# Weighted sum of two expert outputs: tiles of 12 tokens in four buffers in place of 8 in six

## The chip, the core and the metric

The kernel runs on one core of a Trainium2 chip. A core has engines that run beside each other, each with its own queue of instructions in a fixed order: TensorE (PE, not used here), VectorE (DVE), ScalarE (ACT), GpSimd (POOL) and SyncE (SP). Sixteen DMA engines move data between the HBM and the on-chip memory of 128 partitions. The transfers of this kernel are issued from SyncE's queue (q1 in the profile) and from ScalarE's queue (q10); both feed the same sixteen engines. The metric is the time of one execution in microseconds of device time.

## The reference

There are 16 x 1024 tokens; each has two expert outputs of 512 float32 numbers and two weights.

```python
batch, seq, hidden, n_experts, k = 16, 1024, 512, 8, 2
expert_outputs  # (batch, seq, k, hidden) float32, random
combine_weights # (batch, seq, k) float32, random

def reference(expert_outputs, combine_weights):
    weights = combine_weights[..., np.newaxis]
    return np.sum(expert_outputs * weights, axis=2).astype(np.float32)
```

So each output row is `w0 * x0 + w1 * x1`. 67.1 MB of expert outputs are read, 33.6 MB are written, and little is computed on each number.

## The kernel before

The 16384 tokens are spread over 128 partitions, 128 tokens each (`per`). A tile is J = 8 tokens of every partition, so there are 16 tiles, numbered by g. In the first 15 tiles a partition owns 120 consecutive tokens (`main`), whose inputs are 120 x 4 KB = 480 KB apart from those of the next partition; a tile takes 8 consecutive tokens of it, a row of 32 KB. The last tile is laid out by itself: 8 consecutive tokens of each partition, 32 KB apart. `rows` (lines 33 to 37) makes these two views, for inputs, weights and outputs.

The weights are loaded once at the start by two small transfers (lines 53 to 56), the 120 tokens' part from SyncE and the last tile's from ScalarE. One dummy activation on line 59 makes ScalarE load its function table early.

Then, for each tile:

- Line 65: SyncE loads the tile into a buffer `et` of 32 KB per partition. The pool has six such buffers, so the load of tile g+6 is held until the store of tile g has read the buffer.
- Line 70: VectorE multiplies all 16 rows of 512 (8 tokens, two experts) with their weights, in place, in one instruction of 8192 elements per partition.
- Line 71: VectorE adds the two halves of each token and writes the 4096 sums packed into the first half of the same buffer (`ot`).
- Line 72: ScalarE's queue issues the store, one row of 16 KB per partition.

The last tile (lines 75 to 88) is cut by token. ScalarE multiplies the token's first row with its weight (line 77), and VectorE multiplies the second row and adds (line 80). The store is issued from SyncE (line 88), behind all the loads.

The program is written with a tile framework that sets the semaphores and, from its own plan, the order of each engine's instructions. That order is mostly the order of the code, with one exception that matters at the end: on ScalarE two activations of the last tile stand ahead of the stores of tiles 13 and 14, and on VectorE the last multiplies and adds are grouped in pairs. Each queue is served in order: an instruction that waits holds back all behind it on its engine.

A load or a store of a tile is split over the sixteen DMA engines, eight partitions each. A partition's row is one packet. Where both queues have packets for an engine, it takes them in turn.

Of the kernel before, what the change touches and what calls it, by code (L numbers as in the profile page):

```python
# [1 line left out]

# [4 lines left out]


@with_exitstack
def kernel(  # L10
    ctx: ExitStack,
    tc: tile.TileContext,
    expert_outputs: bass.AP,
    combine_weights: bass.AP,
    out: bass.AP,
):

    nc = tc.nc  # L20
    b, s, k, h = expert_outputs.shape
    assert k == 2
    n = b * s
    P = nc.NUM_PARTITIONS
    per = n // P
    assert per * P == n
    J = 8
    main = per - J
    eo = expert_outputs.rearrange("b s k h -> (b s) (k h)")
    cw = combine_weights.rearrange("b s k -> (b s) k")  # L30
    o = out.rearrange("b s h -> (b s) h")

    def rows(x):

        a = x[0 : P * main, :].rearrange("(p t) f -> p t f", p=P)
        b = x[P * main : n, :].rearrange("(p t) f -> p t f", p=P)
        return lambda t, c: a[:, t : t + c, :] if t < main else b[:, t - main : t - main + c, :]

    eo, cw, o = rows(eo), rows(cw), rows(o)

    dt = mybir.dt.float32
    mult = mybir.AluOpType.mult
    add = mybir.AluOpType.add
    copy = mybir.ActivationFunctionType.Copy

    last = per // J - 1

    wpool = ctx.enter_context(tc.tile_pool(name="w", bufs=1))
    ipool = ctx.enter_context(tc.tile_pool(name="in", bufs=6))

    wt = wpool.tile([P, per * k], dt)

    for eng, t, c in ((nc.sync, 0, main), (nc.scalar, main, J)):
        eng.dma_start(  # L54
            out=wt[:, k * t : k * (t + c)].rearrange("p (t k) -> p t k", k=k), in_=cw(t, c)
        )

    warm = wpool.tile([P, 1], dt)
    nc.scalar.activation(out=warm, in_=nc.const_aps.tensor(1.0, (P, 1), dt), func=copy)  # L59

    for g in range(per // J):
        et = ipool.tile([P, J, k * h], dt)

        ot = et.rearrange("p j f -> p (j f)")[:, 0 : J * h].rearrange("p (j f) -> p j f", f=h)
        nc.sync.dma_start(out=et, in_=eo(g * J, J))  # L65
        if g < last:

            wb = wt[:, g * J * k : (g + 1) * J * k].unsqueeze(2).to_broadcast([P, J * k, h])
            ek = et.rearrange("p j (k h) -> p (j k) h", k=k)
            nc.vector.tensor_tensor(out=ek, in0=ek, in1=wb, op=mult)  # L70
            nc.vector.tensor_tensor(out=ot, in0=et[:, :, 0:h], in1=et[:, :, h : 2 * h], op=add)  # L71
            nc.scalar.dma_start(out=o(g * J, J), in_=ot)  # L72
            continue

        for i in range(J):
            t = g * J + i
            nc.scalar.activation(  # L77
                out=et[:, i, 0:h], in_=et[:, i, 0:h], func=copy, scale=wt[:, 2 * t : 2 * t + 1]
            )
            nc.vector.scalar_tensor_tensor(  # L80
                out=ot[:, i, :],
                in0=et[:, i, h : 2 * h],
                scalar=wt[:, 2 * t + 1 : 2 * t + 2],
                in1=et[:, i, 0:h],
                op0=mult,
                op1=add,
            )
        nc.sync.dma_start(out=o(g * J, J), in_=ot)


# [1 line left out]
_INS = ['expert_outputs', 'combine_weights']  # L92
_OUTS = [((16, 1024, 512), 'float32')]


# [23 lines left out]
```

## Time and profile before

| What | Value |
|---|---|
| Median of 3 runs | 240.47 us (240.06 to 240.93) |
| Profiled execution, its own time | 240.47 us |
| Profiled execution, span of the trace | 238.5 us |
| DMA engines, busy share by queue | 68.0% (q1) and 30.9% (q10) |
| VectorE busy | 201.3 us (84%) |
| ScalarE busy | 6.6 us (3%) |
| Transferred | 100.80 MB in 4896 packets, mean 423 GB/s |
| Load of a tile, median from issue to landing | 47.2 us |
| Store of a tile from ScalarE, median from issue to landing | 25.0 us |

The span is what the trace covers, from the first to the last instruction of the execution; the device time is about 2 us longer. A share of the span near 100% on the DMA engines means that they hardly rest. The time from issue to landing includes the time in the queue, so it is many times what the transfer itself takes.

### The profile page before, as it was taken

Reading aid. Unit: us, or ns where it says so; the run is one execution under the profiler, and the core shown is the slowest. Engines: PE = TensorE matmul, PEld = TensorE weight load, DVE = VectorE, ACT = ScalarE, POOL = GpSimd, SP = SyncE. Lnnn points to the kernel's source line nnn. Section 1 sums busy time; section 2 is a strip of 40 time slices with the busy share of each in tenths; the row PEclk is TensorE's granted clock in tenths of the full one; section 3 lists DMA queues with packets and bytes.
Section 4 is the critical chain, followed back from the end, with each engine's and each line's share of the span. In section 5 each row is a group of like instructions: output and inputs, shape, how many; then the busy total and the mean of one; then the engine's idle time right before and its main releaser. Section 6 shows DMA issues by size and latency. Waiting matters only on the chain.

```text
span 238.5 us, 170 instructions
## 1 busy us (share of the span) xinstructions
DVE 201.3 (84%) x38; ACT 6.6 (3%) x10; POOL 0.2 (0%) x4
## 2 busy tenths in 40 slices
DVE  0079999999999998989979799797927999899950
ACT  2000000000000000000000000000000000000530
POOL 0000000000000000000000000000000000000000
DMA  8999989999999999999999999999999999999997
GB/s 286 440 434 429 412 352 437 442 440 451 423 445 393 440 442 440 415 431 467 398 437 473 412 407 473 434 401 431 448 409 426 478 437 401 440 437 404 393 440 308
DMA packets 4896, 100.80 MB, mean 423 GB/s; under 512 B 672, under 2 KB 800, under 8 KB 800
## 3 DMA queue, kind: packets, MB, share of 16 engines
q1 hardware_dynamic: 2592, 69.33, 68.0%
q10 hardware_dynamic: 2304, 31.47, 30.9%
HBM read 67.24 MB, written 33.55 MB: 423 GB/s over the span
## 4 chain that ended last, share of the span: by engine, by line
DMA 65%; DVE 29%; ACT 1%; ACTq 0%; DVEq 0%; issue 0%; SPq 0%
DMA et<-in_expert_outputs_dram 44%; DMA out_dram<-et 21%; DVE et L70 18%; DVE et L71 10%; ACT et L77 1%; DVE et L80 1%; DVEq L114 0%; ACTq L114 0%; SPq L54 0%; ACTq L72 0%; SPq L65 0%; DVEq L80 0%; DVEq L70 0%
## 5 line engine op out<-in xcount | busy, mean ns | idle before, releaser
L70 DVE TENSOR_TENSOR et<-et,wt 128x8192 f32<-128x8192 f32 x15 | 130.4, 8690 | 28.1 <-DMA et<-in_expert_outputs_dram 28.1
L71 DVE TENSOR_TENSOR et<-et 128x4096 f32<-128x4096 f32 x15 | 66.2, 4423 | 0.4
L77 ACT ACTIVATE et<-et,wt 128x512 f32<-128x512 f32 x8 | 5.1, 710 | 220.7 <-DMA et<-in_expert_outputs_dram 218.8
L80 DVE SCALAR_TENSOR_TENSOR et<-et,wt 128x512 f32<-128x512 f32 x8 | 5.6, 748 | 0.2
L59 ACT ACT_TABLE_LOAD x1 | 1.3, 1283 | 1.2 <-PEq L103 1.2
L59 ACT ACTIVATE warm<-const-float32-1.0 128x1 f32<-128x1 f32 x1 | 0.2, 204 | 0.0
L103 POOL MEMSET const-bfloat16-1.0<- 128x1 bf16 x1 | 0.1, 102 | 0.0
L103 POOL MEMSET const-uint8-127<- 128x1 uint8 x1 | 0.1, 102 | 0.0
L103 POOL MEMSET const-float32-0.0<- 128x1 f32 x1 | 0.1, 99 | 0.2 <-issue 0.2
L103 POOL MEMSET const-float32-1.0<- 128x1 f32 x1 | 0.1, 99 | 0.0
## 6 DMA issues: line engine op xcount, KB each, us to landing
et<-in_expert_outputs_dram SPq DMA_DIRECT2D x16, 4096.0 KB, 47.2
out_dram<-et ACTq DMA_DIRECT2D x15, 2048.0 KB, 25.0
out_dram<-et SPq DMA_DIRECT2D x1, 2048.0 KB, 7.6
wt<-in_combine_weights_dram SPq DMA_DIRECT2D x1, 120.0 KB, 2.2
wt<-in_combine_weights_dram ACTq DMA_DIRECT2D x1, 8.0 KB, 2.3
```

The lines of the kernel that those rows point to most:

```text
L59: nc.scalar.activation(out=warm, in_=nc.const_aps.tensor(1.0, (P, 1), dt), func=copy)
L70: nc.vector.tensor_tensor(out=ek, in0=ek, in1=wb, op=mult)
L71: nc.vector.tensor_tensor(out=ot, in0=et[:, :, 0:h], in1=et[:, :, h : 2 * h], op=add)
L77: nc.scalar.activation(out=et[:, i, 0:h], in_=et[:, i, 0:h], func=copy, scale=wt[:, 2 * t : 2 * t + 1])
L80: nc.vector.scalar_tensor_tensor(out=ot[:, i, :], in0=et[:, i, h : 2 * h], scalar=wt[:, 2 * t + 1 : 2 * t + 2], in1=et[:, i, 0:h], op0=mul ...
L103: nc = _bacc.Bacc("TRN2", target_bir_lowering=False, num_devices=1)
```

## The change

Tiles have 12 tokens and there are ten of them; an eleventh, the last, has 8 and is laid out as before. `main` stays 120 and the input rows of neighbouring partitions stay 480 KB apart. A tile's load row becomes 48 KB and its store row 24 KB. The pool has four buffers of 48 KB in place of six of 32 KB, the same 192 KB in all.

The first nine tiles are computed as before, with instructions of 12288 and 6144 elements (lines 72 and 73 of the new file), and stored from ScalarE's queue (line 74). In tile 9 ScalarE multiplies the first rows of its 12 tokens one by one (line 80), VectorE multiplies the second rows in one instruction of 6144 elements (line 95) and adds in another (line 96), and the store is issued from SyncE (line 97). Tile 10 is computed like the old last tile, token by token (lines 80 and 84), and stored from SyncE (line 97).

In the built program, ScalarE's queue holds the stores of tiles 0 to 7, then eight of tile 9's activations, then the store of tile 8, then the other four and the eight of tile 10. SyncE's queue holds all eleven loads, then the stores of tiles 9 and 10. VectorE's order is that of the code, without the pairs.

```diff
-    J = 8
-    main = per - J
+    J, LAST = 12, 8
+    main = per - LAST
+    assert main % J == 0
...
-    last = per // J - 1
+    last = main // J
...
-    ipool = ctx.enter_context(tc.tile_pool(name="in", bufs=6))
+    ipool = ctx.enter_context(tc.tile_pool(name="in", bufs=4))
...
-    for eng, t, c in ((nc.sync, 0, main), (nc.scalar, main, J)):
+    for eng, t, c in ((nc.sync, 0, main), (nc.scalar, main, LAST)):
...
-    for g in range(per // J):
+    for g in range(last + 1):
         et = ipool.tile([P, J, k * h], dt)
...
-        nc.sync.dma_start(out=et, in_=eo(g * J, J))
-        if g < last:
+        t0, c = g * J, J if g < last else LAST
+        nc.sync.dma_start(out=et[:, 0:c], in_=eo(t0, c))
+        if g < last - 1:
...
-            nc.scalar.dma_start(out=o(g * J, J), in_=ot)
+            nc.scalar.dma_start(out=o(t0, c), in_=ot)
             continue
 
-        for i in range(J):
-            t = g * J + i
+
+        for i in range(c):
+            t = t0 + i
             nc.scalar.activation(
                 out=et[:, i, 0:h], in_=et[:, i, 0:h], func=copy, scale=wt[:, 2 * t : 2 * t + 1]
             )
-            nc.vector.scalar_tensor_tensor(
-                out=ot[:, i, :],
-                in0=et[:, i, h : 2 * h],
-                scalar=wt[:, 2 * t + 1 : 2 * t + 2],
-                in1=et[:, i, 0:h],
-                op0=mult,
-                op1=add,
-            )
-        nc.sync.dma_start(out=o(g * J, J), in_=ot)
+            if g == last:
+                nc.vector.scalar_tensor_tensor(
+                    out=ot[:, i, :],
+                    in0=et[:, i, h : 2 * h],
+                    scalar=wt[:, 2 * t + 1 : 2 * t + 2],
+                    in1=et[:, i, 0:h],
+                    op0=mult,
+                    op1=add,
+                )
+        if g < last:
+            w1 = wt.rearrange("p (t k) -> p t k", k=k)[:, t0 : t0 + c, 1:2]
+            x1 = et[:, :, h : 2 * h]
+            nc.vector.tensor_tensor(out=x1, in0=x1, in1=w1.to_broadcast([P, c, h]), op=mult)
+            nc.vector.tensor_tensor(out=ot, in0=et[:, :, 0:h], in1=x1, op=add)
+        nc.sync.dma_start(out=o(t0, c), in_=ot[:, 0:c])
```

## The prediction

> **What bounds the kernel now.** I read the DMA queues and the DMA share first, then the groups by line, then the waits of SyncE, then the end of the timeline. The DMA queues (queue, packets, MB, share of 16 engines' span):
>
> ```profile
> q1 hardware_dynamic: 2592, 69.33, 68.0%
> q10 hardware_dynamic: 2304, 31.47, 30.9%
> HBM read 67.24 MB, written 33.55 MB: 423 GB/s over the span
> ```
>
> The shares add to 98.9%: the 16 DMA engines are the bound. In four stretches (length, busy time of the engines, granted clock, DMA share, GB/s):
>
> ```profile
> 0.00:2.40 2.40, 0.00 (x0) 1.25 (x1) 0.20 (x4) 1.00 0.53 135
> 2.40:219.00 216.60, 190.56 (x29) 0.24 (x2) 0.00 (x0) 1.00 1.00 430
> 219.00:237.30 18.30, 10.79 (x10) 5.12 (x8) 0.00 (x0) 1.00 0.95 402
> 237.30:238.50 1.20, 0.00 (x0) 0.00 (x0) 0.00 (x0) 1.00 0.00 0
> ```
>
> From 2.4 to 219 us no engine rests. Only 2.4 us ahead, 1.2 us behind and 5% of the last 18.3 us (0.9 us) are not transfer. The groups by line (busy us, mean ns, idle before):
>
> ```profile
> L70 DVE TENSOR_TENSOR et<-et,wt 128x8192 f32<-128x8192 f32 x15 | 130.4, 8690 | 28.1 <-DMA et<-in_expert_outputs_dram 28.1
> L71 DVE TENSOR_TENSOR et<-et 128x4096 f32<-128x4096 f32 x15 | 66.2, 4423 | 0.4
> L77 ACT ACTIVATE et<-et,wt 128x512 f32<-128x512 f32 x8 | 5.1, 710 | 220.7 <-DMA et<-in_expert_outputs_dram 218.8
> L80 DVE SCALAR_TENSOR_TENSOR et<-et,wt 128x512 f32<-128x512 f32 x8 | 5.6, 748 | 0.2
> ```
>
> VectorE needs 8.69 + 4.42 = 13.1 us a tile and waits only for loads. The timeline shows the rate of the transfers, one tile in 14.54 us, and the end:
>
> ```profile
> 122.16 8.69 DVE L70 TENSOR_TENSOR et<-et,wt 128x8192 f32<-128x8192 f32 x1 [1.39 <-DMA et<-in_expert_outputs_dram]
> ...
> 136.71 8.69 DVE L70 TENSOR_TENSOR et<-et,wt 128x8192 f32<-128x8192 f32 x1 [1.39 <-DMA et<-in_expert_outputs_dram]
> ...
> 221.50 0.72 ACT L77 ACTIVATE et<-et,wt 128x512 f32<-128x512 f32 x1 [218.84 <-DMA et<-in_expert_outputs_dram]
> 221.56 0.34 ACTq L72 DMA_DIRECT2D out_dram<-et  x1
> ...
> 230.03 0.35 SPq L88 DMA_DIRECT2D out_dram<-et  x1
> ```
>
> The store of tile 13 is issued at 221.56 only because it stands on ScalarE's queue behind two activations that wait for the last load. The packet records show what that costs: the stores before it end at 222.07 on an engine and its first packet starts at 222.40, a hole of about 0.35 us. Then stores run without a break to 237.30, the last one having been issued 2.2 us before its turn.
>
> **The price of packets.** Each partition's row of a tile is one packet (2048 of 32 KB, 2048 of 16 KB among the records), and an engine has 8 of them per transfer. The trace's packet records step by 1.2085 us for 32 KB of load and 0.607 us for 16 KB of store when the queues alternate (8 x 1.8155 = 14.52 us a tile, against 14.54 in the timeline). The difference for 16 KB more is 0.6015 us. So a 48 KB load packet is estimated at 1.810 us and a 24 KB store packet at 0.607 + 0.301 = 0.908 us, and a 12-token tile at 8 x 2.718 = 21.74 us.
>
> **The change part by part.**
>
> *Larger rows.* Per engine now: 128 x 1.2085 + 128 x 0.607 = 232.4 us. After: 80 x 1.810 + 8 x 1.2085 + 80 x 0.908 + 8 x 0.607 = 144.80 + 9.67 + 72.64 + 4.86 = 232.0 us. Gain 0.4 us. The ten transfers fewer (34 become 24) save ten completion writes of 9 ns on each engine, which is 0.1 us more. The Trainium skill (DMA: Bandwidth & Descriptors, "Anatomy of one DMA") gives a DMA a fixed cost of about 2 us besides its bytes. By that rule ten transfers fewer are worth 20 us. The rows speak against it: transfers stand in two queues and the share is 1.00, so the fixed part of one lies under the packets of the others. I take 0.5 us.
>
> *VectorE.* By the same rows (1.042 ns an element, 0.155 us fixed) L70's successor takes 12.95 us and the add 6.55 us, 19.5 together, against 21.74 us of transfer: it stays hidden with 2.2 us a tile to spare.
>
> *The start.* The first load lands later: 2.4 + 0.75 (the first packets are slow now too) + 8 x 1.81 + 0.6 to the semaphore = 18.3 us instead of 13.4. The first store is issued at 18.3 + 19.5 = 37.8 instead of 26.7. Cover: four loads, 58 us of packets, are already queued. Cost 0; without the cover 4.9 us.
>
> *Four buffers for six.* Load g+4 waits for store g. Store 0 is issued at 37.8, starts at 43 (now: issue 26.70, first packet 31.2, since a few load packets are already committed; these are now longer) and is done 21.4 us later; 64.3 with the semaphore. Load 4 is issued then. Loads 1 to 3 last until 72.7, since they share the engines with the stores from 43 on. So load 4 comes 8.4 us before its turn, and in the steady state every round moves on by 21.8 us, so the lead stays: load 7 at 129.6 for 138.1, load 10 at 195.0 for 203.4. Before, that lead was 33 us (load 9 issued at 89.4, first packet 121.9). Cost 0; were the buffer's loop over 8.4 us longer, the excess would be paid about twice (seven reloads on four buffers).
>
> *The end.* On ScalarE the store of tile 8 stands behind eight of tile 9's activations. Load 9 lands at 203.1, eight activations 0.62 us apart (six took 3.78 us) end at 208.1, so this store is issued 7 us after its data are ready (200.9). Behind it on that queue are only the other 12 activations. Store 7 occupies the store queue from 196.2 to 213.1, so nothing waits; loads 9 and 10 run beside it. Tile 9: multiply on VectorE 203.1 to 209.7, add to 216.3 (ScalarE's twelfth activation ends about 211), and I allow 217.7 for its store, issued on SP, which has no load left to issue. Load 10 ends at 219.5 and lands at 220.1. Its eight activations and eight L80-like operations take 6.4 us, as now (5.77 for eight, 0.7 ahead). Its store is issued at 226.5. By 219.5 some three packets of store 8 are out; five are left (4.5 us), and store 9 (7.3 us): the engines are busy until 231.3. The last store's packets are ready at 227.4. So the hole of 0.35 us goes and no new one appears, with 3.9 us in hand. Then 8 x 0.607 = 4.9 us: end at 236.2.
>
> *Sum.* By work: -0.5 (packets) - 0.35 (hole) = -0.85. By the schedule: 236.2 against 237.3 = -1.1. I take -0.9. Profiled execution 240.47 (span 238.5 and 1.97 around it; the median of the runs is the same 240.47): 239.6, span 237.6.
>
> Floor: the skill (the same page, "Where 436 GB/s comes from") puts 435.2 GB/s on the ports. 100.80 MB take 231.6 us by it; with 2.4 and 1.2 around, span 235.2, time 237.2. The 430 GB/s of the long stretch agree. More than 3.3 us cannot be gained; the slow first packets (0.75 us) and a slow change to writing (some 0.65 us near 30 us) stay, so I set the low end at 238.8.
>
> **The rivals.**
>
> *Gain lost, no change.* The packet's fixed part (0.4 us) is a difference of small differences, and the change from reading to writing might cost more with 48 KB packets. Half a microsecond of it leaves 240.1. For it: all terms are below 1 us. Against: the hole is a separate, visible one. Below 0.3% (0.72 us), about what a measurement of this kernel tells from no change, the result is the same.
>
> *Slower: 48 KB rows run at a lower rate.* One mechanism: the longer burst of each partition's row costs more than in proportion. Each 1% on these packets is 80 x 1.81 x 0.01 = 1.45 us. From 0.6% the gain is gone, from 1.1% the kernel is over 0.3% slower; at 2% 239.6 + 2.9 = 242.5. For it: no 48 KB packet is in the trace, and packets at 28 to 32 us took 1.3 to 1.8 us when stores began. [...] Against: the pitch is 480 KB before too, and its packets run at 32 KB / 1.2085 us x 16 = 434 GB/s. I take the row.
>
> *VectorE becomes the bound.* It would need over 21.74 us a tile, 12% more than worked out; each us beyond costs nine: at 24 us a tile 239.6 + 9 x 2.3 = 260. The two rows give the same 1.04 ns an element, so I give it almost nothing.
>
> **How the numbers follow.** Continuous transfer with the gain worked out: 0.70, its own range 238.9 to 240.0; the part of it past 239.75 is 0.14. Gain lost: 0.16 (0.15 same, 0.01 slower). Slower rows: 0.12 (0.11 slower). VectorE or a dry queue: 0.02. Faster 0.56, same 0.30, slower 0.14. The range is 238.8 to 241.2: it leaves out some 0.05 below and 0.13 above.
>
> **What would show it.** Right: 48 KB packets at 1.81 us, the multiplies of L72 21.8 us apart in the timeline once they wait for loads, the DMA share 1.00 from 2.4 us to the end, load 4 issued near 64 us and the last store near 226.5, before the earlier stores have ended. Wrong: 48 KB packets over 1.83 us; a stretch in the middle with a share under 0.98 (loads issued too late); a last store that starts well after the others end.

## The result, and the profile after

| | Kernel before | Changed kernel |
|---|---|---|
| Median of 6 runs each, side by side | 240.5 us (240.06 to 240.95) | 239.89 us (239.26 to 240.61) |
| Ratio to before, 95% interval | 1 | 0.9974 (0.995 to 0.9998) |
| The same in two later groups of runs | 1 | 0.9973 (0.996 to 0.9986), 0.9967 (0.9951 to 0.9983) |
| Profiled execution, its time and span | 240.47, 238.5 us | 239.26, 237.5 us |

The kernel is faster by 0.3%, some 0.6 us; the prediction was 239.6 us, 0.9 us less. The profiled execution of the changed kernel happens to be its fastest. The times of one kernel are spread over more than that gain; the section on what was not expected says what the traces show of that.

The DMA queues after (queue, packets, MB, share of 16 engines' span):

```profile
q1 hardware_dynamic: 2016, 72.48, 71.2%
q10 hardware_dynamic: 1440, 28.32, 27.7%
HBM read 67.24 MB, written 33.55 MB: 424 GB/s over the span
```

The shares add to 98.9% as before, of a span that is 1.0 us shorter. The stretches, cut like those of before but for the last two, which end with this kernel's packets (length, busy time of the engines, granted clock, DMA share, GB/s; a packet is counted whole where it starts, so a share can come out over 1):

```profile
0.00:2.40 2.40, 0.00 (x0) 1.25 (x1) 0.20 (x4) 1.00 0.68 194
2.40:219.00 216.60, 188.40 (x20) 7.70 (x14) 0.00 (x0) 1.00 1.00 430
219.00:236.00 17.00, 5.57 (x8) 5.01 (x8) 0.00 (x0) 1.00 0.99 424
236.00:237.50 1.50, 0.00 (x0) 0.00 (x0) 0.00 (x0) 1.00 0.00 0
```

The long stretch is what it was. The end has gone from a share of 0.95 over 18.3 us to 0.99 over 17.0. The groups by line:

```profile
L72 DVE TENSOR_TENSOR et<-et,wt 128x12288 f32<-128x12288 f32 x9 | 116.6, 12955 | 25.3 <-DMA et<-in_expert_outputs_dram 25.3
L73 DVE TENSOR_TENSOR et<-et 128x6144 f32<-128x6144 f32 x9 | 59.0, 6558 | 0.3
L80 ACT ACTIVATE et<-et,wt 128x512 f32<-128x512 f32 x20 | 12.5, 708 | 210.0 <-DMA et<-in_expert_outputs_dram 210.0
```

12.96 and 6.56 us are what the prediction worked out. The timeline gives the rate of the tiles and the end:

```profile
137.83 12.96 DVE L72 TENSOR_TENSOR et<-et,wt 128x12288 f32<-128x12288 f32 x1 [2.29 <-DMA et<-in_expert_outputs_dram]
...
159.60 12.96 DVE L72 TENSOR_TENSOR et<-et,wt 128x12288 f32<-128x12288 f32 x1 [2.23 <-DMA et<-in_expert_outputs_dram]
...
203.08 0.72 ACT L80 ACTIVATE et<-et,wt 128x512 f32<-128x512 f32 x1 [200.43 <-DMA et<-in_expert_outputs_dram]
203.08 6.56 DVE L95 TENSOR_TENSOR et<-et,wt 128x6144 f32<-128x6144 f32 x1 [2.21 <-DMA et<-in_expert_outputs_dram]
203.18 0.34 ACTq L74 DMA_DIRECT2D out_dram<-et  x1
...
217.16 9.84 SPq L97 DMA_DIRECT2D out_dram<-et  x2
220.09 5.01 ACT L80 ACTIVATE et<-et,wt 128x512 f32<-128x512 f32 x8 [9.55 <-DMA et<-in_expert_outputs_dram]
220.85 5.77 DVE L84 SCALAR_TENSOR_TENSOR et<-et,wt 128x512 f32<-128x512 f32 x8 [3.72 <-ACT et L80]
```

The tiles are 21.77 us apart (21.74 predicted), tile 9 lands at 203.1 (203.1), tile 10 at 220.1 (220.1), and the two stores of L97 are issued at 217.16 (217.7) and 226.65 (226.5). The one step that went otherwise is the store of tile 8: it was issued at 203.18, not 208.1. In the packet records a 48 KB load packet takes 1815 ns, a 24 KB store packet 912, and hardly a record but those around the first load and the first store is slower. The last packet ends at 236.33 us, before at 237.30.

### The profile page after: what moved, and what is told of

It is laid out like the page before. It is cut to its first block, busy times and chain, and to the rows that moved or that the text cites. A ratio compares the mean times of both kernels' runs of the same rounds, so it can differ in the third digit from the quotient of the medians.

```text
span 237.5 us, 153 instructions
## 1 busy us (share of the span) xinstructions
DVE 194.0 (82%) x28; ACT 14.0 (6%) x22; POOL 0.2 (0%) x4
## 3 DMA queue, kind: packets, MB, share of 16 engines
q1 hardware_dynamic: 2016, 72.48, 71.2%
## 4 chain that ended last, share of the span: by engine, by line
DMA 59%; DVE 33%; ACT 2%; DVEq 0%; ACTq 0%; issue 0%; SPq 0%
DMA et<-in_expert_outputs_dram 30%; DMA out_dram<-et 29%; DVE et L72 22%; DVE et L73 11%; ACT et L80 2%; DVE et L84 1%; DVEq L123 0%; ACTq L123 0%; SPq L55 0%; SPq L67 0%; DVEq L72 0%; ACTq L80 0%
## 5 line engine op out<-in xcount | busy, mean ns | idle before, releaser
L72 DVE TENSOR_TENSOR et<-et,wt 128x12288 f32<-128x12288 f32 x9 | 116.6, 12955 | 25.3 <-DMA et<-in_expert_outputs_dram 25.3
L73 DVE TENSOR_TENSOR et<-et 128x6144 f32<-128x6144 f32 x9 | 59.0, 6558 | 0.3
L80 ACT ACTIVATE et<-et,wt 128x512 f32<-128x512 f32 x20 | 12.5, 708 | 210.0 <-DMA et<-in_expert_outputs_dram 210.0
L95 DVE TENSOR_TENSOR et<-et,wt 128x6144 f32<-128x6144 f32 x1 | 6.6, 6558 | 2.2 <-DMA et<-in_expert_outputs_dram 2.2
L96 DVE TENSOR_TENSOR et<-et 128x6144 f32<-128x6144 f32 x1 | 6.6, 6558 | 0.9 <-ACT et L80 0.9
```

The source lines that it names most:

```text
L80: nc.scalar.activation(out=et[:, i, 0:h], in_=et[:, i, 0:h], func=copy, scale=wt[:, 2 * t : 2 * t + 1])
L95: nc.vector.tensor_tensor(out=x1, in0=x1, in1=w1.to_broadcast([P, c, h]), op=mult)
L96: nc.vector.tensor_tensor(out=ot, in0=et[:, :, 0:h], in1=x1, op=add)
```

## The experiments

All of them are edits of the changed kernel, but for the two with shorter rows, which are edits of the kernel before. "Queue theory" in the expectations is the prediction's account: the DMA engines bound the kernel, so its time is that of their packets and of the places where they have none. "Last packet" and "an engine's end" are read from the trace's packet records: while there is work, an engine's packets follow each other within a few ns, so they can be put together to a chain per engine. "The median engine" is the middle of the sixteen ends.

### The tail alone

```diff
-    J, LAST = 12, 8
+    J, LAST = 8, 8
...
-    ipool = ctx.enter_context(tc.tile_pool(name="in", bufs=4))
+    ipool = ctx.enter_context(tc.tile_pool(name="in", bufs=6))
```

> The changed kernel with its 8-token tiles and six buffers back: the new handling of the last two tiles alone. Queue theory (the DMA engines are the bound, the gain is 0.5 us of packet overhead and the closed hole of 0.35 us): the packets are as before (1213 and 611 ns), no hole near 222 us, last packet about 0.4 us earlier than before, 240.1 us. Rival (the gain is all in the rows): 240.5, hole still there. Rival (the gain is all in the tail): 239.6 to 239.9.

Measured: 240.17 us (before, in the same group: 240.78), ratio 0.9978 (0.9965 to 0.9992). The store of tile 13, which the kernel before issued at 221.56, no longer waits for the last load:

```profile
216.17 0.34 ACTq L74 DMA_DIRECT2D out_dram<-et  x1
220.50 8.32 SPq L97 DMA_DIRECT2D out_dram<-et  x2
221.92 5.01 ACT L80 ACTIVATE et<-et,wt 128x512 f32<-128x512 f32 x8 [9.53 <-DMA et<-in_expert_outputs_dram]
```

In the packet records there is no hole near 222 us. The median engine ends at 236.71, against 237.21 in the kernel before and 236.04 to 236.11 in three traces of the changed one. So the traces divide the gain: 0.50 us from the tail, 0.6 to 0.7 us from the rows. The times don't: 0.9978 and 0.9973 have overlapping intervals, and by the medians of this group (240.78 before, 240.17 with the tail alone, 240.23 with the whole change) the tail does as well as the whole. By the fastest execution of each (240.00, 239.84, 239.24) it is mostly in the rows. How much of the measured time each part is worth therefore stays open.

### The rows alone

```diff
-        if g < last - 1:
+        if g < last:
```

> The changed kernel with tile 9 computed by VectorE alone and stored from ScalarE: long rows and four buffers alone. In its built order VectorE's add of tile 9 stands behind the first token of tile 10, which waits for the last load. Queue theory: load 10 lands at 220.1 as in the changed kernel, the token ends at 221.6, the add at 228.1, so store 9 has its first packet at 229.0 while store 8 has ended at about 223.3; a hole of 5.7 us, and the last packet at 236.3 + 4.9 = 241.2; 244.8 us, 2% slower. Rival (the longer rows carry the gain whatever the tail does): 239.6 to 240.1.

Measured: 245.96 us, ratio 1.0195 (1.0169 to 1.0221). The end of its timeline:

```profile
222.02 5.01 ACT L80 ACTIVATE et<-et,wt 128x512 f32<-128x512 f32 x8 [219.36 <-DMA et<-in_expert_outputs_dram]
222.77 0.75 DVE L84 SCALAR_TENSOR_TENSOR et<-et,wt 128x512 f32<-128x512 f32 x1 [4.81 <-ACT et L80]
223.44 6.55 DVE L73 TENSOR_TENSOR et<-et 128x6144 f32<-128x6144 f32 x1
229.91 4.91 DVE L84 SCALAR_TENSOR_TENSOR et<-et,wt 128x512 f32<-128x512 f32 x7
230.03 0.34 ACTq L74 DMA_DIRECT2D out_dram<-et  x1
```

And the stretch of it between the end of store 8 and the start of store 9 (the last two columns are the DMA share and GB/s):

```profile
223.00:231.00 8.00, 7.90 (x4) 4.03 (x7) 0.00 (x0) 1.00 0.17 74
```

The add of tile 9 (L73) stands behind the first token of the last tile, and that one behind the last load: 8 us with a DMA share of 0.17. The order on VectorE is the planner's, not the code's. In this execution the last load landed at 222.0, 1.9 us later than in the changed kernel, which is the rest of the difference to the 244.8 expected (its fastest runs are 244.55 and 244.6). So the larger tiles need the special handling of tile 9: without it they cost 2%.

### One and two activations more for each of the last tokens

```diff
                 out=et[:, i, 0:h], in_=et[:, i, 0:h], func=copy, scale=wt[:, 2 * t : 2 * t + 1]
             )
+            for _ in range(1 if g == last else 0):
+                nc.scalar.activation(out=et[:, i, 0:h], in_=et[:, i, 0:h], func=copy)
```

(2 in place of 1 for the second.)

> The changed kernel with one more activation (a copy onto itself) for each of the last tile's 8 tokens. Each takes ScalarE 0.63 us, so the last store is issued 5.0 us later, at 231.6 instead of 226.6; its packets are ready at 232.5 and the queue runs empty at 231.4. Queue theory (3.9 us in hand): 1.1 us slower than the changed kernel, 241.0. Rival (the chain after the last load sets the end): 5 us slower, 244.9.

> The changed kernel with two more activations (copies onto themselves) for each of the last tile's 8 tokens: the last store is issued 10 us later, at 236.6, ready at 237.5, with the queue empty from 231.4. Queue theory (3.9 us in hand): 6.1 us slower than the changed kernel, 246.0. Rival (the chain after the last load sets the end): 10 us slower, 249.9.

Measured: with one, a median of 240.85 us in the group where the changed kernel had 240.23, and a ratio to before of 0.9979 (0.9957 to 1.0001), not told from the changed kernel's 0.9973. Its times fall into two groups, five from 239.04 to 239.57 us and seven from 240.83 to 241.22, so the median stands for neither; the last section comes back to that. With two, 244.4 us, ratio 1.0149 (1.0108 to 1.0191), some 4.2 us over the changed kernel of the other group. Both came out faster than the 241.0 and 246.0 expected: a copy takes 0.54 us (four in 2.17), not 0.63.

The last store of the first was issued 10.1 us after the last load had landed, 3.6 us later than in the changed kernel (6.6), which is less than the time in hand; so that the faster five lost nothing (the changed kernel's fastest is 239.24) is what the account asks for. The last store of the second came 7.84 us later (234.49 against 226.65), not 10. Its stretches:

```profile
219.00:231.00 12.00, 4.17 (x6) 10.78 (x20) 0.00 (x0) 1.00 0.99 426
231.00:235.50 4.50, 1.57 (x3) 2.53 (x5) 0.00 (x0) 1.00 0.14 58
235.50:240.40 4.90, 0.00 (x0) 0.00 (x0) 0.00 (x0) 1.00 0.89 375
```

The engines run dry between 230.9 and 231.6 and take up again at 235.3. The last packet ends at 240.41, 4.08 us later than in the changed kernel: of 7.84 us, 3.76 were covered. The prediction had put 3.9 us in hand.

### Three buffers

```diff
-    ipool = ctx.enter_context(tc.tile_pool(name="in", bufs=4))
+    ipool = ctx.enter_context(tc.tile_pool(name="in", bufs=3))
```

> The changed kernel with three buffers of 48 KB instead of four. The prediction's own reading (a load's lead of 8.4 us is all the slack there is, the excess is paid at each round of the buffers): one buffer fewer takes 21.7 us off the round, 13.3 us over the lead, eight reloads on three buffers, +36 us, 276 us. Queue theory in full (a store that waits in its queue behind the one before it is slack too, 6 to 17 us of it): the stores start soon after their issue, both queues stay fed but for about 1.5 us near 55 us, and the last load lands near 226 instead of 220; 2 to 3 us slower than the changed kernel, 242 to 243 us.

Measured: 251.31 us, ratio 1.0432 (1.0396 to 1.0468). Both expectations missed, the one by 8 to 9 us, the other by 25. Four of its stretches:

```profile
54.00:58.00 4.00, 4.00 (x2) 0.00 (x0) 0.00 (x0) 1.00 0.68 209
58.00:168.00 110.00, 96.54 (x10) 0.00 (x0) 0.00 (x0) 1.00 0.99 420
168.00:170.00 2.00, 0.27 (x1) 0.00 (x0) 0.00 (x0) 1.00 0.69 295
...
214.00:218.00 4.00, 2.56 (x1) 2.56 (x5) 0.00 (x0) 1.00 0.61 156
```

The records account for the 11.0 us by which its last packet (247.36) is later than the changed kernel's. An engine rests for 5.4 us in the mean, most of it at 54 to 58 and at 214 to 218. And the packets are slower: 7.0 us per engine over the usual durations, against 1.4 in the changed kernel. That happens at each of the places where a queue had run empty and starts again (near 41, 57, 130, 148, 175 and 217 us); there the slowest 48 KB packets take 2.3 to 3.3 us instead of 1.8, and at 217, where the last load starts, the slowest of its 32 KB packets 2.7 instead of 1.2. A share of 0.99 hides this part: a slow packet is a busy engine. Neither expectation had a price for starting again.

### Four short buffers

```diff
-    J, LAST = 12, 8
+    J, LAST = 8, 8
```

> The changed kernel with 8-token tiles in four buffers: half the bytes on chip that six buffers hold, less by a third than the changed kernel's. Queue theory, with the sizes of the runs so far: a buffer's round is 4 x 14.54 = 58.2 us; what it needs is some 4 us from a load's issue to its first packet behind committed packets, 14.5 for the load, 0.6 to the semaphore, 13.1 on VectorE, 4.5 from the store's issue to its first packet, 14.5 for the store and 1.5 to the semaphore, 52.7 us. 5 us are left, so no queue runs empty and the time is that of the 8-token kernel with six buffers, 240.2 us, ratio 0.997 to 0.999. Rival (each buffer taken away is paid, as with three of 48 KB): 3 us or more slower than that, 243 and up, with slow packets and holes in the middle of the trace.

Measured: 241.37 us, ratio 1.0035 (1.001 to 1.006), 0.6% over the same kernel with six buffers, where queue theory had expected no difference (240.2) and the rival 243 and up: neither is met. In the middle the expectation of the queues holds: the share is full and no packet is slow.

```profile
40.00:190.00 150.00, 134.27 (x20) 0.00 (x0) 0.00 (x0) 1.00 1.01 433
190.00:212.00 22.00, 22.00 (x5) 5.01 (x8) 0.00 (x0) 1.00 0.99 427
212.00:231.00 19.00, 14.31 (x11) 5.01 (x8) 0.00 (x0) 1.00 1.00 429
231.00:233.00 2.00, 0.34 (x1) 0.00 (x0) 0.00 (x0) 1.00 0.96 410
```

The loss is at the end. The planner puts VectorE's last instructions in pairs (two multiplies, then two adds), so store 11 starts only at 199.0; load 15, which waits for it, starts at 212.4 where loads could have run from 205.2, and its last packet is at 223.75 (220.93 with six). After that the last store comes too late for the others: 12 of the engines have a hole near 232, of 0.1 to 0.6 us. The trace is of one of the faster executions (241.12; they go up to 243.72), so this part of the loss is shown and the rest of the 1.2 us over the kernel with six buffers (240.17) is not.

### Shorter rows

```diff
-    J = 8
+    J = 4
...
-    ipool = ctx.enter_context(tc.tile_pool(name="in", bufs=6))
+    ipool = ctx.enter_context(tc.tile_pool(name="in", bufs=12))
```

(J = 2 and bufs=24 for the second.)

> The kernel before with 4-token tiles in twelve buffers: rows of 16 KB and 8 KB, 66 transfers instead of 34. Queue theory: 256 packets more on each engine at 6 ns of fixed part, 1.5 us, and 32 completion writes at 9 ns, 0.3 us: 242.3 us. Rival (a fixed 2 us for each transfer, which the larger tiles save): 32 x 2 = 64 us more, 304 us.

> The kernel before with 2-token tiles in 24 buffers: rows of 8 KB and 4 KB, 130 transfers. Queue theory: 768 packets more on each engine at 6 ns, 4.6 us, and 96 completion writes at 9 ns, 0.9 us: 246.0 us, if the transfers in flight still fill the queues. Rival (a fixed 2 us for each transfer): 192 us more, 432 us.

Measured: 241.65 us, ratio 1.0041 (1.0025 to 1.0056), and 245.37 us, ratio 1.0188 (1.0168 to 1.0208); 1.0 and 4.7 us over before where 1.8 and 5.5 were expected. The queues of the second:

```profile
q1 hardware_dynamic: 9504, 67.77, 66.4%
q10 hardware_dynamic: 9216, 33.04, 33.2%
```

Its 130 transfers keep the engines at 99.6% of the span. The records of all kernels make one line: 159 ns for 4 KB, 309 for 8, 611 for 16, 912 for 24, 1213 for 32, 1815 for 48. Doubling 4 KB gives 318, 9 ns more than 8 KB take; doubling 8 KB 618, 7 ns more than 16. That is the fixed part of a packet. The rival's 2 us for each transfer, 64 and 192 us, is 40 to 70 times what 32 and 96 transfers more cost here.

### The first load ahead of the weights

```diff
-    for eng, t, c in ((nc.sync, 0, main), (nc.scalar, main, LAST)):
+    for eng, t, c in ((nc.scalar, 0, main), (nc.scalar, main, LAST)):
```

> The changed kernel with both weight transfers on ScalarE's queue, so that SyncE's first issue is the load of tile 0, at 0.73 us instead of 1.16. If the order of the issues sets when the engines start in earnest: first load packets near 1.8 instead of 2.3, everything 0.4 us earlier, 239.8 against 240.2. Queue theory: the engines start at 1.73 in both, and the weights' 0.55 us of packets are still to be moved, only beside the load; 0 to 0.1 us, ratio as the changed kernel's, 0.996 to 0.998.

Measured: 239.88 us, ratio 0.9949 (0.9931 to 0.9967). The queue theory had allowed 0 to 0.1 us; the trace has the last packet at 235.93 (236.33), the start of tile 0's multiply at 18.27 us (18.43). Its first stretches, and that multiply:

```profile
0.00:2.40 2.40, 0.00 (x0) 0.76 (x1) 0.20 (x4) 1.00 1.06 328
2.40:219.00 216.60, 188.34 (x20) 8.18 (x14) 0.00 (x0) 1.00 1.00 429
...
18.27 12.96 DVE L72 TENSOR_TENSOR et<-et,wt 128x12288 f32<-128x12288 f32 x1 [18.27 <-DMA wt<-in_combine_weights_dram]
```

The engines begin at 1.73 to 1.75 us in both kernels, but now with load packets, which at the start take 2.3 to 2.7 us here (2.2 to 2.9 in the changed kernel) instead of 1.8. In the changed kernel the weights stand ahead: an engine's first load packet starts at 2.3 to 2.9 us. Here they are not ahead of the load but take turns with it, one small packet after each load packet. That costs each engine 0.44 us of packets in place of 0.48 to 0.56, but the weights of the first 120 tokens arrive only with tile 0 itself (last packet at 17.67 us, tile 0's at 17.63), and those of the last tile at 32.23. It is now the weights that the first multiply waits for. It was run again beside the changed kernel:

> The changed kernel beside the one that issues load 0 first, on the same chip, to compare these two directly. Start theory (the weights' packets, 0.55 us on each engine, lie ahead of the first load here and hide under its slow first packets there): 0.3 to 0.45 us more than the other, a ratio to the kernel before of 0.996 to 0.998. Rival (the start makes no difference): the two within 0.1 us.

> The changed kernel with both weight transfers on ScalarE's queue, once more and beside the changed kernel. Start theory: first load packets at 1.75 us, last packet at 235.9 to 236.1 on most engines, 0.3 to 0.45 us less than the changed kernel, ratio to the kernel before 0.994 to 0.996. Rival (the start makes no difference): within 0.1 us of the changed kernel.

Measured: 240.18 us for the changed kernel, ratio 0.9967 (0.9951 to 0.9983), and 239.59 us, ratio 0.9946 (0.9927 to 0.9964). Twice the same: this version is 0.5% under the kernel before, and beside the changed kernel 0.6 us or 0.2% under it. The median engine ends at 235.75 and 235.90 in its two traces, at 236.04, 236.11 and 236.10 in the three of the changed kernel, so 0.1 to 0.4 us are in the records; the intervals of the two ratios overlap a little (0.9951 to 0.9964). By its ratios it is the fastest kernel here.

### The changed kernel once more

> The changed kernel itself, for a second trace and a narrower interval. Queue theory: the sum of its terms, 0.9 us less than before, ratio 0.996; last load at 220, last store issued at 226.6 and last packet at 236.3 to 236.5 whatever the time of the execution. Rival (the first trace was a lucky one): ratio 0.998 to 1.000, with slower packets or a hole somewhere that the first trace does not show.

Measured: 240.23 us, ratio 0.9973 (0.996 to 0.9986). Both expectations are right in part. The packets and their order are those of the first trace, and the median engine ends at 236.11. But one engine ends at 237.44, the last load lands at 222.1 in place of 220.1, the last store is issued at 228.65, and the span is 238.6. The last section tells of that.

## Why the prediction was right

**What bounds the kernel.** The DMA engines, all the time: every kernel here whose queues stay filled runs at a share of 0.99 to 1.01 and ends when its packets are out. VectorE waits for loads in both kernels.

**Larger rows.** Predicted 1.810 and 0.908 us a packet and 0.5 us in all; measured 1815 and 912 ns in the records, 21.77 us for a tile, and 0.6 to 0.7 us between the tail alone and the changed kernel on the median engine. The rule of 2 us per transfer was rightly set aside. The Trainium skill (DMA: Bandwidth & Descriptors, "Anatomy of one DMA") gives it for transfers issued from GpSimd, and those here are issued from SyncE and ScalarE; the two kernels with shorter rows paid 0.03 and 0.05 us for each transfer more, packets included. The rival that 48 KB rows run slower fell on the first record: 1815 ns for nearly all 1280 packets.

**The hole.** Predicted 0.35 us, read from one engine. Over all sixteen the records of the kernel before have holes of 0 to 0.7 us, 0.45 in the mean, and the tail alone gives 0.50 us on the median engine.

**Four buffers for six.** Predicted at nothing, with load 4 issued at 64.3 and started at 72.7; measured 64.28 and 72.48. This is right for this kernel. The price given if the cover were gone (the excess paid about twice) was wrong: with three buffers the loss was 11 us, made of waiting and of slow starts, and no excess of a round times a number of rounds gives it.

**The end.** The schedule's landing, issue and last packet were met within 0.6 us in the first trace (in the two with a late engine, of which the last section tells, the landing came about 2 us later and the last packet 1.1 and 1.8), and the 3.9 us in hand are 3.76 in the run that used them up. The step that failed is the hold of store 8 on ScalarE: it was said to wait until eight activations end. It waits until the first can start. At 203.18, 0.10 us after the first of the eight began, the store was issued; the queue hands activations on without awaiting their end. The same stood in the profile of before (the activation at 221.50, the store behind it at 221.56) and was not read. It cost nothing, since store 7 held the store queue until 212.1.

**The sum.** -0.9 predicted. The packets of the median engine say 236.10 - 237.21 = -1.1. The profiled executions say -1.2, but there the fastest of the changed kernel stands against a middle one of the kernel before; fastest against fastest, the three groups say -0.80, -0.76 and -0.70, and their medians -0.61, -0.55 and -0.69. So by the traces both gains were put too small, and by the times the sum is too large. That it came out so near owes something to luck: what the two gains have too little, a term that the prediction does not have takes back. The traces show a candidate, an engine that lags (last section). That it is what the medians lack is argued and not shown: the kernel before is spread as widely (240.00 to 241.67 us in one group), and of it there is one trace.

## What to carry to other kernels

When the transfers fill the span, predict with the packets: their number times their duration per engine, then the places where a queue can run empty. A slack is worth a number: write down how long before its turn each transfer is issued, and what remains to be sent when the last one becomes ready. Fewer and larger tiles at the same memory are nearly free in the middle and dangerous at the end, where a planner's order of one add cost 2%; and small transfers that the first tile needs cost less beside its load, on the other queue, than ahead of it (0.1 to 0.4 us on the median engine here), as long as they arrive with it. A hole read from one trace can be that execution's own.

## What the runs showed of the hardware that was not expected

**One late engine of sixteen.** In the first trace of the changed kernel all engines end between 235.83 and 236.33 us. In the second 15 end by 236.62 and one at 237.44; in the third 14 by 236.43 and two at 237.95 and 238.17; in the second trace of the version with the first load ahead 15 by 236.17 and one at 237.23. These executions took 240.37, 241.10 and 240.16 us, those without a late engine 239.26 and 238.88. The records of the second trace show where it comes from: between 20 and 60 us, when the first stores meet the loads, the late engine's packets take 1.55 us over their usual durations, those of the others 0.5 to 0.9. From 60 to 210 us no packet of any engine is slow there, so nothing is made up: each engine moves its own partitions, and the end and every landing wait for the last one. Why one engine is hit and not another is not known.

The lag shows more plainly where the last store comes too late anyway. One activation more for each token gave times in two groups (239.04 to 239.57 and 240.83 to 241.22 us), so did two (243.52 and 243.58, 245.22 and 245.36) and the rows alone (244.55 and 244.60, 245.83 to 246.20). The traces of the first and the last are from the slower group and have three late engines and one (1.6 to 1.8 and 1.55 us between 20 and 60 us), the trace of the second is from the faster one and has none. That the untraced executions divide in the same way is an inference.

In the trace of the kernel before, the last load's packets end between 219.40 and 219.76 us on 14 engines, at 219.95 and 220.39 on the other two, and yet all engines end within 0.16 us of each other (237.14 to 237.30). The hole takes the lag up, since an early engine waits longer in it; in the trace with one activation more, 2.2 us shrink to 0.17 in the same way. But the store behind the hole waits for the last landing, so the lag also makes the hole. An estimate from these figures: had all engines been done by 219.76, the store of tile 13 would have been issued near 220.9 and started near 221.8, before the stores ahead of it ended (221.84 to 222.38). So the hole that the change closes may be that execution's own, and closing it worth less in others; by the fastest executions the tail alone gains 0.16 us. A second trace of the kernel before would tell, and there is none.

**A start costs.** Packets that are first after a queue has been empty take mostly 1.2 to 1.8 times as long (48 KB: 2.2 to 2.9 us at the start of the changed kernel, up to 3.3 with three buffers).

**A first store waits.** From the issue of the first store to its first packet it took 4.5 us in the kernel before (26.70 to 31.2) and 5.4, 3.8 and 4.8 in the three traces of the changed one (38.02 to 43.4 in the first) while loads were running, though the two queues alternate from then on. Where only stores were left it took 0.84 us (221.56 to 222.40). That load packets which the engines had already taken stand ahead of the store is the prediction's reading, and no run here tests it.
